# Transposed input, an early first product and adding DMAs in a seven-product projection on Trainium2

## The chip, the cores and the metric

The kernel runs on one core of a Trainium2 chip. The metric is the device time of one execution in microseconds. The core has TensorE (PE, matrix products into PSUM, with the weight load PEld as a row of its own), VectorE (DVE), ScalarE (ACT), GpSimd (POOL) and SyncE (SP). PE adds in eight PSUM banks of 128 x 512 floats. SP, ACT and POOL also issue DMAs; each of these queues is worked off in order, and all transfers run on the same 16 DMA engines.

## The reference

A decoder trunk of two layers over 512 tokens of width 2048, all in float32. Layer 0 is gated linear attention (GLA) with four heads, layer 1 latent attention (MLA) with 16 heads. Each layer is

```python
h = rms_norm(x, g_pre)
y = mixer(h, ...)                # one wide projection of h, attention, gate, w_out
x = x + rms_norm(y, g_post)
```

The change lies mostly in the first projection of layer 0:

```python
proj = h @ w_in                                   # 512 x 2048 times 2048 x 6160
q, k, v, gate, gk_low = jnp.split(proj, ...)      # 1024, 1024, 2048, 2048, 16 columns
gk = gk_low @ w_gk2 + b_gk
log_a = log_sigmoid(gk) / 16                      # the decays, summed up within chunks
```

Scores are made of q and k weighted by the exponents of the summed decays; the scores times v are normed per head, multiplied by silu(gate), and go through `w_out`.

## The kernel before

Every float32 product is made of three in the faster format fp32r: a number is split into a high part (rounded on ACT) and a low part (the rest, on DVE), and `mm3` (lines 128 to 132) adds high x high, low x high and high x low into one bank.

The wide projection is cut into six blocks m of 1024 columns, two halves n1 and n2 of 512 each: (q, k) of heads 0 and 1, (v, gate) of heads 0 and 1, then the same for heads 2 and 3. Each block is one 2 x 2 block product with seven multiplications instead of eight. The two halves on the side of x are the token halves and, within each pair kp of 128-row pieces of the 2048, the even and the odd piece; on the side of the weights they are the even and odd piece and n1 and n2. The seven products need sums of pieces on both sides. The left sums live in `act_hi` and `act_lo`, in four slots for each pair; the right sums are made anew while the weights stream in.

The slots hold only four of the seven left operands. So there are two stages:

1. `first_four` (line 253): for all six blocks, four products with eight banks, 8 pairs kp of 24 matmuls. SP loads two pieces left (n1) and two right (n2), 512 KB each, three buffers of either; DVE makes three sums, ACT and DVE split four pieces. The results are combined and written to the DRAM tensor `stage` through POOL.
2. `left_rest` (line 374) makes the other left operands from `ht`, the transposed normed input in SBUF.
3. `last_three` (line 286): for each block three products with six banks, 18 matmuls a pair; one reload of `stage` (`done`, 1.5 MB, POOL); the result goes to `evac`. q and k are transposed and multiplied by the decay factors (`qk_evac`, line 579), then `scores` (616), `values` (657) follow for each head. The decays are made by `gk_spread` (510) and `decays` (538) when stage 2 begins and again after the second head.

Before all that, `start` (line 320) loads the rows of x, norms them (ACT squares, DVE scales), transposes them on PE (line 353), copies them to `ht`, splits them, and makes the left sums. `constants` (390) and `gk_low` (498: 32 float32 matmuls of the gate's low rank) follow, then the first block. Results of the heads go through DRAM (`yd`) and are transposed by `gla_rows` (674). `out_proj` (689) makes the output projection in column blocks of 512, the last 512 as two blocks of 256, the second with its weights kept in SBUF; `mla` does the same with the first latent projection (lines 779 to 783: two halves of 256 columns).

The order on each engine comes from a planner: the program is traced, and a scheduler puts each engine's instructions and DMA queue in order by a simulated timeline before it is built (`tc` with `schedule_with_timeline_sim=True`, line 1056). On the chip each queue keeps that order and waits by semaphores. SBUF is handed out by pools that open on the left or on the right side and lie behind one another; a tile that takes over the place of an earlier pool's tile waits until that tile is no longer read.

Of the kernel before, what the change touches and what calls it, by code (L numbers as in the profile page):

```python
# [14 lines left out]
F32 = DT.float32  # L15
# [8 lines left out]
P = 128  # L24
# [21 lines left out]
NMAC = 6  # L46
GQ0, GK0, GV0, GG0, GL0 = 0, 1024, 2048, 4096, 6144
# [3 lines left out]
R_BGK, R_GON, R_GQA, R_GKV, R_PRE = 0, 8, 12, 16, 20  # L51
NROWS = 36
# [23 lines left out]
class Trunk:  # L76
# [121 lines left out]
    def build(self):  # L198
        tc, a = self.tc, self.a
        from contextlib import ExitStack  # L200
        with ExitStack() as ctx:
# [18 lines left out]
            self.gla_rows()  # L220
# [18 lines left out]
    def raw_pair(self, w, c0, kp, rows=2, name="raw"):  # L239

        t = self.wp.tile([P, rows, 512], F32, tag=f"{name}{rows}", name=name, bufs=3)
        src = w[(2 * kp + 2 - rows) * P:(2 * kp + 2) * P, c0:c0 + 512]
        self.nc.sync.dma_start(t, src.rearrange("(k p) n -> p k n", p=P))
        return t

    def prods(self, ps, kp, slots, hi, lo, ws):
        for q, (slot, wi) in enumerate(zip(slots, ws)):
            for r in range(2):
                self.mm3(ps[2 * q + r], self.act_slot(self.act_hi, kp, slot, r),
                         self.act_slot(self.act_lo, kp, slot, r), hi[:, wi, :], lo[:, wi, :],  # L250
                         kp == 0, kp == KT // 2 - 1)

    def first_four(self, w, m, n1, n2):


        nc, v = self.nc, self.nc.vector
        ps = [self.ps.tile([P, 512], F32, tag="a", name=f"pa{q}", bufs=8) for q in range(8)]
        for kp in range(KT // 2):
            r1 = self.raw_pair(w, n1, kp, name="left")
            r2 = self.raw_pair(w, n2, kp, name="right")  # L260
            t = self.wp.tile([P, 3, 512], F32, tag="sums", name="sums", bufs=2)
            v.tensor_tensor(t[:, 0, :], r1[:, 0, :], r2[:, 0, :], ALU.add)
            v.tensor_tensor(t[:, 1, :], t[:, 0, :], r2[:, 1, :], ALU.add)
            v.tensor_tensor(t[:, 2, :], t[:, 1, :], r1[:, 1, :], ALU.add)
            hi = self.wp.tile([P, 4, 512], FR, tag="w_hi", name="w_hi", bufs=2)
            lo = self.wp.tile([P, 4, 512], FR, tag="w_lo", name="w_lo", bufs=2)
            nc.scalar.copy(hi[:, 0, :], r1[:, 0, :])
            v.tensor_tensor(lo[:, 0, :], r1[:, 0, :], hi[:, 0, :].bitcast(F32), ALU.subtract)
            nc.scalar.copy(hi[:, 1:4, :], t)  # L269
            v.tensor_tensor(lo[:, 1:4, :], t, hi[:, 1:4, :].bitcast(F32), ALU.subtract)  # L270
            self.prods(ps, kp, (0, 2, 1, 3), hi, lo, (0, 2, 1, 3))
        for r in range(2):
            p1 = self.stg([P, 512], "p1")
            nc.scalar.copy(p1, ps[r])  # L274
            nc.gpsimd.dma_start(self.stage[m, :, 0, r, :], p1)
            u = self.stg([P, 512], "u2")
            v.tensor_tensor(u, p1, ps[2 + r], ALU.subtract)
            for i, p in ((1, ps[4 + r]), (2, ps[6 + r])):
                t = self.stg([P, 512], "vw")
                v.tensor_tensor(t, u, p, ALU.add)  # L280
                nc.gpsimd.dma_start(self.stage[m, :, i, r, :], t)

# [3 lines left out]
    def last_three(self, w, m, n1, n2, evac):  # L286


        nc, v = self.nc, self.nc.vector
        ps = [self.ps.tile([P, 512], F32, tag="b", name=f"pb{q}", bufs=6) for q in range(6)]  # L290
        done = self.sp.tile([P, 3, 2, 512], F32, tag="done", name="done", bufs=1)
        nc.gpsimd.dma_start(done, self.stage[m])
        for kp in range(KT // 2):
            r1 = self.raw_pair(w, n1, kp, 1, name="left")
            r2 = self.raw_pair(w, n2, kp, name="right")
            t = self.wp.tile([P, 512], F32, tag="sum", name="sum", bufs=2)
            v.tensor_tensor(t, r2[:, 0, :], r2[:, 1, :], ALU.add)
            hi = self.wp.tile([P, 3, 512], FR, tag="w_hi", name="w_hi", bufs=2)
            lo = self.wp.tile([P, 3, 512], FR, tag="w_lo", name="w_lo", bufs=2)
            for i, x in enumerate((r1[:, 0, :], r2[:, 1, :], t)):  # L300
                nc.scalar.copy(hi[:, i, :], x)
                v.tensor_tensor(lo[:, i, :], x, hi[:, i, :].bitcast(F32), ALU.subtract)  # L302
            self.prods(ps, kp, (2, 0, 1), hi, lo, (0, 1, 2))
        for r in range(2):
            p2, q3, p7 = ps[r], ps[2 + r], ps[4 + r]
            c = [self.stg([P, 512], f"c{i}") for i in range(4)]
            v.tensor_tensor(c[0], p2, done[:, 0, r, :], ALU.add)
            evac(r, 0, c[0])
            v.tensor_tensor(c[1], q3, done[:, 1, r, :], ALU.subtract)
            evac(r, 1, c[1])  # L310
            v.tensor_tensor(c[2], p7, done[:, 2, r, :], ALU.add)
            evac(2 + r, 0, c[2])
            v.scalar_tensor_tensor(c[3], p7, -1.0, done[:, 1, r, :], ALU.mult, ALU.subtract)
            evac(2 + r, 1, c[3])
# [5 lines left out]
    def start(self):  # L320

        nc, v, a, cp = self.nc, self.nc.vector, self.a, self.cp
        xs = a["x"][0]
        tc = self.tc
        cf = cp.tile([P, P + 1], F32, name="cf")
        self.ident, self.invf = cf[:, 0:P], cf[:, P:P + 1]
        self.eps = cp.tile([P, 1], F32, name="eps")
        nc.vector.memset(self.eps, EPS)
        self.junk = cp.tile([P, 512], BF16, name="junk")
        with tc.tile_pool(name="start", bufs=1, reuse_waits="tile") as xp:  # L330
            xt = []
            for s in range(ST):
                x = xp.tile([P, D], F32, tag="x", name=f"x{s}", bufs=3)
                for g in range(4 if s == 0 else 1):
                    c = slice(g * 512, (g + 1) * 512) if s == 0 else slice(0, D)
                    nc.sync.dma_start(x[:, c], xs[s * P:(s + 1) * P, c])
                if s == 0:
                    nc.scalar.dma_start(cf, a["consts"])
                    gr = xp.tile([P, D], F32, tag="grow", name="grow")
                    nc.scalar.dma_start(gr, a["l0_pre_norm"][None, :].to_broadcast([P, D]))  # L340
                xt.append(x)
            for s in range(ST):
                parts = self.st.tile([P, 4], F32, tag="parts", name="parts", bufs=2)
                for g in range(4):
                    self.sumsq(xt[s][:, g * 512:(g + 1) * 512], parts[:, g:g + 1])
                rstd = self.rstd_of(self.total(parts, "x_ssq"), D, "x_rstd")
                cols = slice(s * P, (s + 1) * P)
                for g in range(4):
                    c = slice(g * 512, (g + 1) * 512)
                    v.scalar_tensor_tensor(xt[s][:, c], xt[s][:, c], rstd, gr[:, c], ALU.mult, ALU.mult)  # L350
                    pt = self.ps.tile([P, 512], F32, tag="a", name="xn_t", bufs=8)
                    for j in range(4):
                        nc.tensor.transpose(pt[:, j * P:(j + 1) * P],
                                            xt[s][:, (4 * g + j) * P:(4 * g + j + 1) * P], self.ident)
                    pv = pt.rearrange("p (k n) -> p k n", n=P)
                    nc.scalar.copy(self.ht[:, 4 * g:4 * g + 4, cols], pv)
                    ks = slice(4 * g + s // 2, 4 * g + 4, 2)
                    self.split_from(pv[:, s // 2::2, :], self.act_hi[:, ks, cols], self.act_lo[:, ks, cols])
            for g in range(4):
                self.left_sums(xp, g)  # L360

    def left_sums(self, pool, g):

        nc, v = self.nc, self.nc.vector
        h = lambda odd, half: self.ht[:, 4 * g + odd:4 * g + 4:2, half * 256:(half + 1) * 256]
        x = pool.tile([P, 2, 2, 256], F32, tag="lsum", name="lsum", bufs=2)
# [5 lines left out]
        v.tensor_tensor(sl(self.act_lo), x, sl(self.act_hi).bitcast(F32), ALU.subtract)  # L372

    def left_rest(self, g):

        nc, v = self.nc, self.nc.vector
        h = lambda odd, half: self.ht[:, 4 * g + odd:4 * g + 4:2, half * 256:(half + 1) * 256]
        x = self.tp.tile([P, 2, 2, 256], F32, tag="lsum", name="lsum", bufs=2)
        v.tensor_tensor(x[:, :, 0, :], h(1, 1), h(0, 1), ALU.subtract)
# [81 lines left out]
    def gla(self):  # L461
# [8 lines left out]
        with pool("ht", **R) as hp:  # L470
# [9 lines left out]
            with pool("lb", **R) as self.tp:  # L480
                for g in range(4):
                    self.left_rest(g)
# [577 lines left out]
```

## Time and profile before

| | |
|---|---|
| median of 3 runs | 1564.92 us (1564.27 to 1565.75) |
| the profiled execution, its span | 1565.73 us, 1564.0 us |
| first product matmul of `first_four` | 72.7 us |
| last product matmul of `first_four` | 337.3 us |
| heads done, transposes of `gla_rows` begin | 656 us |
| granted PE clock, mean | 0.967 |
| DMA | 216.09 MB, mean 138 GB/s |

The page of the profile has busy times by engine, the span in 40 slices, the queues, the chain of work that ended last, and groups of equal instructions. A window row gives, for a stretch of the span, the busy time of each engine with its number of instructions, the granted PE clock, the mean busy share of the DMA engines, and what they moved. Matmuls overlap in the records: one of 512 columns is shown as 0.39 us, though a new one starts every 0.23 us. So the rate is the stretch divided by the number of matmuls. A wait row names who waited for what: total, times, longest. A group's row ends with the idle time ahead of it and what ended it. A DMA row has the median time from issue to landing.

### The profile page before, as it was taken

How to read it: one execution, taken by the hardware profiler on the slowest of the kernel's cores; microseconds unless marked ns; L12 is line 12 of the kernel's file. 1: busy time of each engine (PE TensorE's matmuls, PEld its weight loads, DVE VectorE, ACT ScalarE, POOL GpSimd, SP SyncE). 2: the span in 40 equal slices, each digit the busy share in tenths (PEclk: the TensorE clock that was granted, in tenths of full speed). 3: DMA queues.
4: the chain of work that ended last, by engine and by line, in shares of the span. 5: the costliest groups of instructions: out<-in, count | busy, mean ns of one | idle time of the engine just before them, and what ended most of it. 6: DMA issues, size and time to landing. Idle time of an engine off the chain costs nothing.

```text
span 1564.0 us, 19919 instructions
## 1 busy us (share of the span) xinstructions
PE 1463.3 (94%) x7409; PEld 1234.4 (79%) x7409; DVE 978.1 (63%) x1652; ACT 729.7 (47%) x1391; POOL 68.6 (4%) x130
## 2 busy tenths in 40 slices
PE   2699999978699799699999999999999999999998
PEld 2287887857588678588899988888888889888888
DVE  6488888879888878544347434344367777863324
ACT  6233343335366446534336424444466666753221
POOL 0200000001000000200001100000000000000000
PEclk7799999999899989799999999999999999999999
DMA  7167777745366555744326223333322221235222
GB/s 283 29 181 223 229 226 226 223 166 188 121 199 192 167 168 163 256 132 126 111 88 227 71 81 105 98 95 94 82 72 70 60 60 51 69 124 171 94 95 108
DMA packets 132961, 216.09 MB, mean 138 GB/s; under 512 B 19628, under 2 KB 56720, under 8 KB 130048
## 3 DMA queue, kind: packets, MB, share of 16 engines
q1 hardware_dynamic: 124064, 178.81, 37.4%
q0 software_dynamic: 8512, 34.89, 6.5%
q8 instruction: 58, 0.95, 0.3%
q10 hardware_dynamic: 288, 1.11, 0.2%
q14 instruction: 39, 0.32, 0.1%
HBM read 192.53 MB, written 22.25 MB: 137 GB/s over the span
## 4 chain that ended last, share of the span: by engine, by line
PE 70%; issue 18%; DVE 6%; DMA 3%; ACT 2%; POOL 1%; SPq 0%; DVEq 0%; POOLq 0%; ACTq 0%
PE yo_acc L130 8%; PE yo_acc L132 8%; PE yo_acc L131 8%; PE pb L130 4%; PE pb L131 4%; PE pb L132 3%; PE acc L132 3%; PE acc L131 3%; PE acc L130 3%; PE q_acc L132 1%; PE q_acc L131 1%; PE q_acc L130 1%; PE pt L1012 1%; DMA right<-in_l_gla_w_in_dram 1%; PE cq_acc L131 1%
## 5 line engine op out<-in xcount | busy, mean ns | idle before, releaser
L131 PE MATMUL yo_acc<-w_hi,act_lo 128*128 128x512 f32 (+1 forms) x440 | 154.1, 351 | 0.0
L132 PE MATMUL yo_acc<-w_lo,act_hi 128*128 128x512 f32 (+1 forms) x440 | 153.0, 349 | 0.0
L130 PE MATMUL yo_acc<-w_hi,act_hi 128*128 128x512 f32 (+1 forms) x440 | 152.8, 349 | 0.0
L130 PE MATMUL pa<-w_hi,act_hi 128*128 128x512 f32 x384 | 150.4, 392 | 1.4 <-ACT p L274 1.4
L131 PE MATMUL pa<-w_hi,act_lo 128*128 128x512 f32 x384 | 149.5, 389 | 0.0
L124 DVE SCALAR_TENSOR_TENSOR w_lo<-w_raw,gcol,w_hi 128x512 fp32r<-128x512 f32 (+1 forms) x98 | 64.6, 698 | 106.6 <-ACT w_hi L123 106.5
L130 PE MATMUL pb<-w_hi,act_hi 128*128 128x512 f32 x288 | 116.4, 408 | 12.7 <-ACT act_hi L384 7.6
L132 PE MATMUL pa<-w_lo,act_hi 128*128 128x512 f32 x384 | 118.3, 389 | 0.0
L123 ACT ACTIVATE w_hi<-w_raw,gcol 128x512 fp32r<-128x512 f32 (+1 forms) x98 | 61.5, 676 | 114.0 <-PE acc L132 83.9
L131 PE MATMUL pb<-w_hi,act_lo 128*128 128x512 f32 x288 | 114.0, 397 | 0.0
L132 PE MATMUL pb<-w_lo,act_hi 128*128 128x512 f32 x288 | 101.0, 398 | 0.8 <-DVE w_lo L302 0.8
L130 PE MATMUL acc<-act_hi,w_hi 128*128 128x512 f32 x256 | 99.7, 389 | 0.0
L131 PE MATMUL acc<-act_hi,w_lo 128*128 128x512 f32 x256 | 99.6, 389 | 0.0
L132 PE MATMUL acc<-act_lo,w_hi 128*128 128x512 f32 x256 | 99.1, 389 | 0.0
L270 DVE TENSOR_TENSOR w_lo<-sums,w_hi 128x1536 fp32r<-128x1536 f32 x48 | 84.2, 1754 | 15.1 <-ACT w_hi L269 15.1
L130 PEld LDWEIGHTS yo_acc<-w_hi,act_hi 128*128 128x128 f32 x440 | 83.7, 190 | 10.5 <-ACT act_hi L179 0.2
L131 PEld LDWEIGHTS yo_acc<-w_hi,act_lo 128*128 128x128 f32 x440 | 83.7, 190 | 10.0
L132 PEld LDWEIGHTS yo_acc<-w_lo,act_hi 128*128 128x128 f32 x440 | 83.6, 190 | 10.0
L116 DVE TENSOR_TENSOR w_lo<-w_raw,w_hi 128x1024 fp32r<-128x1024 f32 x32 | 39.2, 1224 | 80.9 <-ACT w_hi L115 80.8
L130 PEld LDWEIGHTS pa<-w_hi,act_hi 128*128 128x128 f32 x384 | 72.0, 188 | 20.5 <-ACT p L274 3.2
L124 DVE SCALAR_TENSOR_TENSOR w_lo<-w_raw,gon,w_hi 128x512 fp32r<-128x512 f32 (+1 forms) x80 | 47.7, 641 | 59.6 <-ACT w_hi L123 59.3
L132 PEld LDWEIGHTS pa<-w_lo,act_hi 128*128 128x128 f32 x384 | 72.1, 188 | 15.0
(331 smaller groups left out, 3636.9 us busy)
## 6 DMA issues: line engine op xcount, KB each, us to landing
right<-in_l_gla_w_in_dram SPq DMA_DIRECT2D x96, 512.0 KB, 4.3
left<-in_l_gla_w_in_dram SPq DMA_DIRECT2D x48, 512.0 KB, 4.7
w_raw<-in_l_mla_w_in_dram SPq DMA_DIRECT2D x47, 512.0 KB, 3.7
w_raw<-in_l_gla_w_out_dram SPq DMA_DIRECT2D x32, 512.0 KB, 4.0
w_raw<-in_l_mla_w_out_dram SPq DMA_DIRECT2D x32, 512.0 KB, 3.6
left<-in_l_gla_w_in_dram SPq DMA_DIRECT2D x48, 256.0 KB, 3.6
done<-stage POOLq DMA_DIRECT2D x6, 1536.0 KB, 7.4
pw_raw<-in_l_mla_w_kvb_dram SPq DMA_DIRECT2D x64, 128.0 KB, 2.6
```

Source lines behind the costliest of these rows:

```text
L116: nc.vector.tensor_tensor(lo, raw, hi.bitcast(F32), ALU.subtract)
L123: nc.scalar.activation(hi[:, kk, :], raw[:, kk, :], AF.Copy, scale=g)
L124: nc.vector.scalar_tensor_tensor(lo[:, kk, :], raw[:, kk, :], g, hi[:, kk, :].bitcast(F32), ALU.mult, ALU.subtract)
L130: t.matmul(out, lh, rh, start=start, stop=False)
L131: t.matmul(out, ll, rh, start=False, stop=False)
L132: t.matmul(out, lh, rl, start=False, stop=stop)
L270: v.tensor_tensor(lo[:, 1:4, :], t, hi[:, 1:4, :].bitcast(F32), ALU.subtract)
L1012: te.transpose(pt[:, o:o + P], probs[i][:, j * P:(j + 1) * P], self.ident)
```

## The change

1. **Input.** The program gets x transposed (`xt`) and all gains as columns, laid out ahead of the launch. `start` loads `xt` by 128-row pieces, even ones first, and multiplies by the gain. The row norm isn't applied to x any more; its factors (`rcol`) are made by `x_norm` after block 0 and are multiplied in where q, k, v and the gate leave the projection, and into the low-rank gate.
2. **Early product.** The first of the seven products (even pieces, first token half, n1) is formed for blocks 0, 1 and 2 by `first_one`, as pieces of `xt` and weights come in, ahead of the left sums. For these blocks `first_four` makes three products, and four for the others.
3. **Adding DMAs.** One sum of weight pieces in either stage is made by a DMA from POOL that adds a 256 KB piece from DRAM onto the loaded one in SBUF.
4. **Order.** `gk_low`, `gk_spread` and the first `decays` come after block 1; the sums for the second stage are made in place in `ht` after block 3 (`left_swap`), so `left_rest` only splits. Both heads' scores follow q and k at once. `stage` is reloaded in pieces of 256 KB. The transposes of the heads move into the second stage (`y_rows`), the last head's straight from SBUF. `ht` moves to the left side of SBUF.
5. **Widths.** The last 512 columns of `out_proj` and the first latent projection are one block of 512 columns, halved along the 2048 instead.

The core of the diff:

```diff
+    def first_one(self, w, n1, rows=None):
+        ps = [self.bank("a", f"p1_{r}") for r in range(2)]
+        wr = w[:, n1:n1 + 512].rearrange("(k p) n -> p k n", p=P)
+        for g in range(4):
+            t = self.wp.tile([P, 2, 512], F32, tag="left", name="left", bufs=3)
...
+            wt = self.split_w(t)
+            for i in range(2):
+                self.prod(ps, 2 * g + i, 0, wt, i)
+        return ps
+    def first_four(self, w, m, n1, n2, p1=None):
+        have = p1 is not None
+        ps1 = None if have else [self.bank("t", f"p1_{r}") for r in range(2)]
+        ps = [self.bank("a", f"pa{q}") for q in range(6)]
+        for kp in range(KT // 2):
+            left = self.raw_pair(w, n1, kp, "left")
+            right = self.raw_pair(w, n2, kp, "right")
+            if DMA_ADD:
+                nc.gpsimd.dma_start(right[:, 0, :], w[2 * kp * P:(2 * kp + 1) * P, n1:n1 + 512], accum_op=ALU.add)
+            else:
+                v.tensor_tensor(right[:, 0, :], left[:, 0, :], right[:, 0, :], ALU.add)
+            v.tensor_tensor(right[:, 1, :], right[:, 0, :], right[:, 1, :], ALU.add)
+            wr = self.split_w(right)
+            v.tensor_tensor(left[:, 1, :], right[:, 1, :], left[:, 1, :], ALU.add)
+            if have:
...
+                nc.scalar.copy(hi[:, 1, :], left[:, 1, :])
+                v.tensor_tensor(lo[:, 1, :], left[:, 1, :], hi[:, 1, :].bitcast(F32), ALU.subtract)
+                wl = hi, lo
+            else:
+                wl = self.split_w(left)
+                self.prod(ps1, kp, 0, wl, 0)
+            self.prod(ps[0:2], kp, 2, wr, 1)
+            self.prod(ps[2:4], kp, 1, wr, 0)
+            self.prod(ps[4:6], kp, 3, wl, 1)
     def last_three(self, w, m, n1, n2, evac):
-        nc.gpsimd.dma_start(done, self.stage[m])
         for kp in range(KT // 2):
+            t = self.wp.tile([P, 3, 512], F32, tag="raw", name="raw", bufs=3)
...
+            if self.dma_add:
+                nc.gpsimd.dma_start(t[:, 1, :], w[odd, n2:n2 + 512], accum_op=ALU.add)
+            else:
+                v.tensor_tensor(t[:, 1, :], t[:, 1, :], t[:, 2, :], ALU.add)
+            wt = self.split_w(t)
...
+        def done(i, r):
+            t = self.sp.tile([P, 512], F32, tag="done", name="done", bufs=4)
+            nc.gpsimd.dma_start(t, self.stage[m, :, i, r, :])
+            return t
     def start(self):
+        def even(k):
+            nc.sync.dma_start(self.ht[:, k, :], xt[:, k, :])
+            nc.scalar.activation(self.act_hi[:, k, half], self.ht[:, k, half], AF.Copy, scale=gain(k))
+            v.scalar_tensor_tensor(self.act_lo[:, k, half], self.ht[:, k, half], gain(k),
+                                   self.act_hi[:, k, half].bitcast(F32), ALU.mult, ALU.subtract)
+        p1 = [self.first_one(w, self.order[0][0], even)]
+        for g in range(4):
+            ks = slice(4 * g + 1, 4 * g + 4, 2)
+            nc.sync.dma_start(self.ht[:, ks, :], xt[:, ks, :])
+        for m in (1, 2):
+            p1.append(self.first_one(w, self.order[m][0]))
+            for g in (2 * m - 2, 2 * m - 1):
+                for k in range(4 * g, 4 * g + 4):
+                    nc.scalar.activation(self.ht[:, k, :], self.ht[:, k, :], AF.Copy, scale=gain(k))
+                self.left_sums(g)
+    def x_norm(self):
+        for s in range(ST):
+            for g in range(4):
+                t = self.tmp([P, 512], F32, "x")
+                nc.gpsimd.dma_start(t, self.a["x"][0, s * P:(s + 1) * P, g * 512:(g + 1) * 512])
+                self.sumsq(t, parts[:, s, g:g + 1])
...
     def gla(self):
+            with pool("ht") as hp, pool("wa") as self.wp, pool("psa", space=PS) as self.ps:
+                    early = [self.p1_out(m, ps) for m, ps in enumerate(early)]
                     for m, (n1, n2) in enumerate(order):
+                        self.first_four(w, m, n1, n2, early[m] if m < len(early) else None)
+                        if m == 0:
+                            self.x_norm()
+                            self.constants()
+                        if m == 1:
+                            self.gk_low()
+                            self.gk_spread()
+                            with tc.issue_after(self.ln_exp.ins):
+                                self.decays(0)
+                        if m == 3:
+                            for g in range(4):
+                                self.left_swap(g)
+                    for g in range(4):
+                        self.left_rest(g)
+                for p in range(2):
+                    self.last_three(w, 3 * p, *qk(p), self.qk_evac)
+                    at = [self.scores(h) for h in (2 * p, 2 * p + 1)]
+                    if p == 0:
+                        self.decays(1)
+                    for i, h in enumerate((2 * p, 2 * p + 1)):
+                        self.last_three(w, 3 * p + 1 + i, *vg(h), self.vg_begin(h))
+                        if h == GH - 1:
+                            for e in range(h):
+                                self.y_rows(e)
+                        self.values(h, at[i])
+                self.y_rows(GH - 1)
     def out_proj(self, w, gpost, y_of, then, ahead=None, gain=None):
-        self.block_s(w, 1536, 256, 0, ps, hi, lo, KT, gain=gain, evac=evac(3, 1536, 256, 0))
-        self.block_s(w, 1792, 256, 256, ps, hi, lo, KT, gain=gain, evac=evac(4, 1792, 256, 256), resident=True)
+        self.block_s(w, 1536, 512, 0, ps, hi, lo, KT, gain=gain, ks=(0, KT // 2))
+        self.block_s(w, 1536, 512, 0, ps, hi, lo, KT, gain=gain, evac=evac(3, 1536, 512, 0), resident=True,
+                     ks=(KT // 2, KT))
```

`split_w` copies a tile to `w_hi` on ACT and subtracts for `w_lo` on DVE; `prod` is the six matmuls of one product for one pair; `bank` hands out six banks of tag "a" and two of tag "t".

More of the change, by code (lines that the diff above doesn't have):

```diff
@@ new lines, in split_w, with prod @@
+    def split_w(self, t):
+        nc = self.nc
+        shape = list(t.shape)
+        hi = self.wp.tile(shape, FR, tag="w_hi", name="w_hi", bufs=self.w_bufs)
+        lo = self.wp.tile(shape, FR, tag="w_lo", name="w_lo", bufs=self.w_bufs)
+        nc.scalar.copy(hi, t)
+        nc.vector.tensor_tensor(lo, t, hi.bitcast(F32), ALU.subtract)
+        return hi, lo
+    def prod(self, ps, kp, slot, wt, i):
+        for r in range(2):
+            self.mm3(ps[r], self.act_slot(self.act_hi, kp, slot, r),
+                     self.act_slot(self.act_lo, kp, slot, r), wt[0][:, i, :], wt[1][:, i, :],
+                     kp == 0, kp == KT // 2 - 1)
@@ new lines, in first_four @@
+    def first_four(self, w, m, n1, n2, p1=None):
+        nc, v = self.nc, self.nc.vector
+        have = p1 is not None
[12 more added lines that the diff above has]
+            if have:
+                hi = self.wp.tile([P, 2, 512], FR, tag="w_hi", name="w_hi", bufs=self.w_bufs)
+                lo = self.wp.tile([P, 2, 512], FR, tag="w_lo", name="w_lo", bufs=self.w_bufs)
+                nc.scalar.copy(hi[:, 1, :], left[:, 1, :])
[7 more added lines that the diff above has]
+            self.prod(ps[4:6], kp, 3, wl, 1)
+        if not have:
+            p1 = self.p1_out(m, ps1)
+        u = []
+        for r in range(2):
+            u.append(self.stg([P, 512], "u2"))
+            v.tensor_tensor(u[r], p1[r], ps[r], ALU.subtract)
+        for i in (1, 2):
+            for r in range(2):
+                t = self.stg([P, 512], "vw")
+                v.tensor_tensor(t, u[r], ps[2 * i + r], ALU.add)
+                nc.gpsimd.dma_start(self.stage[m, :, i, r, :], t)
@@ L317, in tmp0 @@
+        d = [done(1, r) for r in range(2)]
+        for r in range(2):
+            t = c()
+            v.tensor_tensor(t, ps[2 + r], d[r], ALU.subtract)
+            evac(r, 1, t)
+        for r in range(2):
+            p7 = ps[4 + r]
+            t = c()
+            v.tensor_tensor(t, p7, done(2, r), ALU.add)
+            evac(2 + r, 0, t)
+            t = c()
+            v.scalar_tensor_tensor(t, p7, -1.0, d[r], ALU.mult, ALU.subtract)
+            evac(2 + r, 1, t)
     def tmp0(self, shape, dtype, name):
@@ L329, in start @@
         self.junk = cp.tile([P, 512], BF16, name="junk")
[L330 to L360, printed above, removed]
@@ L1050 @@
     given.update(_constants())
+    given.update(_laid_out(given))
     arrays, a = {}, {}
```

299 lines of the change are left out of this document (145 added, 154 removed).

## The prediction

> **What bounds the kernel now.** I read the page first, then windows cut at the stages, then PE's waits, then the timeline and the groups where an edit has a price.
>
> ```profile
> span 1564.0 us, 19919 instructions
> PE 1463.3 (94%) x7409; PEld 1234.4 (79%) x7409; DVE 978.1 (63%) x1652; ACT 729.7 (47%) x1391; POOL 68.6 (4%) x130
> ...
> core 0: us, PE busy (x) PEld busy (x) DVE busy (x) ACT busy (x) POOL busy (x), PEclk, DMA share, GB/s
> 0.00:72.70 72.70, 30.55 (x98) 16.39 (x98) 43.52 (x86) 37.07 (x84) 8.33 (x19) 0.74 0.49 168
> 72.70:337.30 264.60, 263.18 (x1153) 214.97 (x1152) 215.62 (x261) 101.04 (x108) 17.77 (x33) 1.00 0.68 207
> 337.30:356.00 18.70, 7.00 (x15) 4.49 (x16) 14.52 (x24) 5.89 (x9) 2.15 (x4) 0.69 0.46 155
> 356.00:632.00 276.00, 250.67 (x1128) 204.14 (x1128) 230.22 (x388) 147.30 (x289) 18.57 (x34) 0.95 0.56 175
> 632.00:658.00 26.00, 13.46 (x36) 9.07 (x34) 16.62 (x29) 16.41 (x40) 5.76 (x11) 0.68 0.62 220
> 658.00:1564.00 906.00, 898.48 (x4984) 785.33 (x4984) 457.61 (x869) 421.95 (x863) 16.03 (x30) 1.00 0.33 102
> 195.00:234.00 39.00, 39.00 (x173) 31.87 (x172) 33.06 (x41) 15.76 (x17) 3.23 (x6) 1.00 0.73 222
> 1519.00:1549.00 30.00, 30.00 (x252) 30.00 (x252) 13.04 (x26) 6.88 (x19) 0.00 (x0) 1.00 0.18 66
> 4.00:24.00 20.00, 5.74 (x26) 5.34 (x27) 9.44 (x18) 13.85 (x41) 0.00 (x0) 0.90 1.02 399
> ```
>
> TensorE (PE) bounds it wherever it is fed. The first four products of all six blocks (72.7 to 337.3) run 1152 matmuls in 264.6 us, 0.2297 us each, at full clock. From 658 on PE is also full. The loose time is in three places: the start (72.7 us), the change of stage at 337, and the second stage to 658. The waits name them.
>
> ```profile
> PE xn_t L353 <- DVE x L350: 27.4, 4, 13.0
> PE qk_t L584 <- DVE eq L588: 23.2, 4, 11.0
> PE pb L130 <- ACT act_hi L384: 7.6, 1, 7.6
> PE y_t L683 <- DMA y<-yd: 4.3, 1, 4.3
> ...
> 337.30:354.70 17.40, 5.74 (x12) 3.43 (x12) 0.00 (x0) 0.70 0.49 167
> 384.00:416.00 32.00, 13.10 (x49) 9.41 (x47) 5.20 (x8) 0.79 0.24 73
> 530.00:560.00 30.00, 13.22 (x53) 9.69 (x52) 4.67 (x7) 0.77 0.29 95
> ```
>
> The last three rows count only the product matmuls (pb). Twelve are worth 2.8 us of the 17.4, so 14.6 us are lost at the change of stage. The other two windows hold 49 and 53, worth 11.3 and 12.2; even with some 4 us of transposes in each, about 17 and 14 us are lost, where the decays are computed between q, k and the scores.
>
> **The change, part by part.** The profiled execution took 1565.7 us, 1.7 over its span and 0.8 over the median of the runs; the sum is made against it.
>
> *Start.* Row norms, transposes of x and their waits leave the path. x^T is 4.2 MB (16 x 128 x 512 x 4 bytes), the weights of one early product 2.1 MB, so 10.5 MB come before block 0's own weights: 26 us at the 399 GB/s of 4 to 24 us. PE needs 3 x 48 x 0.2297 = 33.1 us for the three early products and so hides that.
>
> ```profile
> x<-in_x_dram SPq DMA_DIRECT2D x4, 256.0 KB, 7.6
> L267 ACT CAST w_hi<-left 128x512 fp32r<-128x512 f32 x48 | 29.9, 624 | 103.6 <-PE pa L131 103.6
> L268 DVE TENSOR_TENSOR w_lo<-left,w_hi 128x512 fp32r<-128x512 f32 x48 | 33.1, 689 | 38.8 <-ACT w_hi L267 27.0 <-PE pa L131 8.1 <-PE pa L132 2.5
> L274 ACT COPY p<-pa 128x512 f32<-128x512 f32 x12 | 7.0, 581 | 30.9 <-DMA stage<-p 22.2 <-DVE sums L263 4.4 <-PE pa L132 4.3
> 61.42 11.32 PE L504 MATMUL gkl_acc<-ht,gkl_raw 128*16 128x512 f32 x26
> ```
>
> The first matmul waits 7.6 + 0.6 + 0.7 = 8.9 us; with 33.1 and six copies that free the banks (6 x 0.58 = 3.5), block 0 proper starts at 45.5. The gains and the left sums on ScalarE (ACT) and VectorE (DVE) hide under products one and two. The low-rank gate's 32 matmuls of 0.435 us (13.9) and 2 us for the decays move into the stage; half is charged (8), since they fit into the stalls below. The removed transposes were on no full PE.
>
> *Adding DMAs.* Now every pair of row blocks passes through three buffers: load, adding DMA (a), remaining adds, split, release. DVE's add that goes is worth nothing by itself: DVE is busy 215.6 of 264.6 us and PE is full. The new wait sits on POOL: behind an add wait stage writes, reloads and the x loads; for it wait DVE, ACT and PE. On SP the next left load, and the right one behind it, wait for the release.
>
> ```profile
> right<-in_l_gla_w_in_dram SPq DMA_DIRECT2D x96, 512.0 KB, 4.3
> left<-in_l_gla_w_in_dram SPq DMA_DIRECT2D x48, 512.0 KB, 4.7
> gkl_raw<-in_l_gla_w_in_dram POOLq DMA_DIRECT2D x1, 128.0 KB, 4.1
> DMA to landing us min/median/max: 3.4/8.0/11.0
> L115 ACT CAST w_hi<-w_raw 128x1024 fp32r<-128x1024 f32 x32 | 33.7, 1054 | 80.2 <-PE yo_acc L131 76.2 <-DMA w_raw<-in_l_mla_w_out_dram 3.5 <-PE q_acc L132 0.4
> L116 DVE TENSOR_TENSOR w_lo<-w_raw,w_hi 128x1024 fp32r<-128x1024 f32 x32 | 39.2, 1224 | 80.9 <-ACT w_hi L115 80.8
> L269 ACT CAST w_hi<-sums 128x1536 fp32r<-128x1536 f32 x48 | 71.0, 1479 | 22.8 <-DVE sums L264 22.8
> L270 DVE TENSOR_TENSOR w_lo<-sums,w_hi 128x1536 fp32r<-128x1536 f32 x48 | 84.2, 1754 | 15.1 <-ACT w_hi L269 15.1
> ```
>
> No row shows an adding DMA. The nearest are POOL's loads from DRAM: 4.1 us for 128 KB, and 3.4 (shortest) to 8.0 us (median) for the 256 KB loads of x in the output stage, the fourth row. I take a = 5.0, near the lower ones because the 8.0 holds queueing behind siblings, and above them because an add must also fetch what it adds to; 3.4 and 8.0 stay as bounds. A negative price is excluded: the load must land first.
>
> Blocks 0 to 2: 4.7 + a + 0.69 + 1.05 + 1.22 + 0.69 + 0.62 + 0.69 = 9.66 + a, so 14.7 over three buffers, 4.89 us a pair, against 18 x 0.2297 = 4.13 for PE. Blocks 3 to 5 split one piece more on each engine: 10.6 + a = 15.6, 5.2 against 24 x 0.2297 = 5.51, hidden. The stage then ends at 45.5 + 24 x 4.89 + 24 x 5.51 + 8 = 303.1 instead of 337.3: **-34.2**.
>
> The Trainium skill ("DMA: Bandwidth & Descriptors", Anatomy of one DMA) fits a DMA from GpSimd as 2.0 us plus bytes over 436e3, an estimate of 2.6 us for 256 KB; the trace's POOL loads are longer. By it the sum would be about 1480.
>
> *Second stage.* Its chain is 4.7 + a + 1.48 + 1.75 = 12.9, 4.31 us a pair against 4.13: 48 x 0.18 = 8.6, half covered by scores and values: **+4**. The decays of heads 0 and 1 move into the first stage, those of 2 and 3 beside v and g. Of the 31 us lost in the two windows I take 26 back; what is late next is the evacuation of q and k, now with a ScalarE scaling, for which the next block's products are the cover: **-26** (bounds -20 and -31). At the end of the stage three of four heads are transposed early and the last comes straight from SBUF: the 4.3 us wait and part of the 26 us window with 36 matmuls go, **-10** (-4 to -15). The change of stage stays: ht now lies on the left, where I read the second stage's weight tiles to be placed, so their loads wait until the last split of ht (1.48 + 1.75) is done; then 4.3 + 5 + 1.48 + 1.75, 15.8 us and a cold clock: **+2** (if the places don't collide -11).
>
> *POOL's queue.* 16 x loads through three buffers and 36 single reloads instead of six stand in it with the adds.
>
> ```profile
> L281 POOL DMA_DIRECT2D stage<-vw x24 | 13.0, 540 | 39.2 <-DVE vw L280 39.2
> POOL done L292 <- DVE c L313: 179.1, 5, 41.0
> ```
>
> Issuing is cheap (0.54 us). But a reload waits for a free buffer, up to 41 us in one piece, and an add behind it would wait along: **+8** (0 to +49, below).
>
> *Wider pieces.* 252 matmuls of 256 columns take 30.0 us (0.1190 each), 173 of 512 take 39.0 (0.2254). 1152 of the first become 576 of the second (768 in the two output projections, 384 in the latent q): 576 x (0.2380 - 0.2254) = **-7.3**.
>
> By the Trainium skill ("TensorE: Matmul & The Clock Gate", Back-to-back issue gap) an isolated warm matmul takes N / 2.4 + 2.5 ns, which leaves 2.5 ns a pair, 1.5 us in all. The trace has 12.6, and weight loads busy all 30.0 of 30.0 us say why. By the rule the sum would be 1508.
>
> Sum: -34.2 - 26 - 10 + 2 + 8 + 4 - 7.3 = -63.5, so **1502 us**.
>
> **Rivals.**
>
> *The add is slow, and the three buffers become the bound (slower).* With a = 8: blocks 0 to 2 cost 17.7 / 3 = 5.89 (+24), blocks 3 to 5 6.2 (+17), the second stage 5.31, uncovered since PE's order is fixed ahead (+53), the change of stage +1: +95 in all, 1597 us. It decides from a of about 7.0. For it: the 8.0 median. Against it: DMA share 0.68 in that stage, and the 128 KB at 4.1.
>
> *Blocked queue.* Adds work, but a reload at the head of POOL's queue holds the next block's first add until the old block is evacuated; PE then waits a + 1.48 + 1.75 = 8.2 us in each of six blocks, 49 instead of 8: 1543. For it: the 179.1 us that POOL waited for that release. Against it: the planner orders each queue by a simulated timeline, in which an add that is ready goes first.
>
> *Cheap add.* a = 3.4 and no blocking: 24 x 0.53 = 13, 4 and 8 us less: 1477. For it: the shortest x load.
>
> **How the numbers follow.** The forecast (1485 to 1525) gets 0.52, the cheap add 0.17, the blocked queue 0.15, the slow add 0.13, and 0.03 is left for a cancellation within 0.2% (3 us), about what a measurement of this kernel can tell. Faster are the first three, 0.84. The range from 1475 to 1560 holds them nearly whole and leaves out the slow add and the rest, about 0.2.
>
> **What would show it.** The first product matmul by 10 us and block 0's own by 45; a pair in blocks 0 to 2 near 4.9 us and in 3 to 5 near 5.5; adds landing in 4 to 6 us; the last first-stage matmul near 303; the 11 us waits of qk_t gone; a gap of some 16 us at the change of stage; no 256-column matmuls in the output projections. Adds of 7 us or more, or SP waiting for the adds' tiles while PE idles all through both stages, would make it wrong.

## The result and the profile after

The changed kernel takes 1629.14 us (median of 4 runs, 1622.57 to 1635.33). The kernel before took 1565.34 us (1564.27 to 1566.08) beside it. The ratio is 1.0408 (95% interval 1.0366 to 1.0449): slower, where the forecast was 1502 us and the range ended at 1560. The profiled execution took 1622.6 us.

The page of the changed kernel, with the totals, the two main DMA queues, the engines' shares of the chain of work that ended last, and loads of the two stages with the median time to landing (`raw` is the second stage's tile; a row from POOLq is an adding DMA):

```profile
span 1620.8 us, 18861 instructions
PE 1479.2 (91%) x6776; PEld 1209.1 (75%) x6776; DVE 890.8 (55%) x1402; ACT 727.7 (45%) x1261; POOL 171.3 (11%) x263
...
q1 hardware_dynamic: 122288, 184.06, 36.9%
q0 software_dynamic: 25152, 63.19, 16.8%
...
PE 62%; DMA 20%; DVE 8%; ACT 5%; issue 4%; SPq 0%; POOL 0%; DVEq 0%; POOLq 0%; ACTq 0%
...
left<-in_l_gla_w_in_dram SPq DMA_DIRECT2D x59, 512.0 KB, 5.8
right<-in_l_gla_w_in_dram SPq DMA_DIRECT2D x48, 512.0 KB, 5.3
...
right<-in_l_gla_w_in_dram POOLq DMA_DIRECT2D x48, 256.0 KB, 5.5
...
raw<-in_l_gla_w_in_dram POOLq DMA_DIRECT2D x48, 256.0 KB, 5.7
```

DVE is relieved as meant. The adds (last two rows) land in 5.5 and 5.7 us, but the loads from SP have become slower too: 5.8 and 5.3 us for left and right, where the kernel before had 4.7 and 4.3. DMA holds 20% of the chain.

Windows of the changed kernel, cut at the first and last product matmul of either stage:

```profile
core 0: us, PE busy (x) PEld busy (x) DVE busy (x) ACT busy (x) POOL busy (x), PEclk, DMA share, GB/s
20.00:40.00 20.00, 19.97 (x59) 7.80 (x58) 18.15 (x27) 19.19 (x35) 2.45 (x5) 1.00 0.72 247
68.80:386.50 317.70, 262.52 (x1028) 205.86 (x1027) 198.64 (x265) 112.55 (x124) 60.96 (x86) 0.91 0.80 211
386.50:402.60 16.10, 0.44 (x3) 0.02 (x1) 4.15 (x6) 2.13 (x3) 5.33 (x9) 0.64 0.90 277
402.60:694.30 291.70, 259.39 (x1145) 208.93 (x1146) 178.55 (x220) 136.43 (x200) 65.97 (x94) 0.96 0.84 221
694.30:1620.80 926.50, 906.09 (x4436) 763.41 (x4434) 467.99 (x857) 430.00 (x853) 20.39 (x38) 0.99 0.33 100
```

The first stage, where PE was full before, now has PE idle for 55 us. The DMA share is 0.80 and 0.84 in the two stages, where it was 0.68 and 0.56. The forecast can be cut in the same way: its second stage is 631.1 (before's last matmul there) - 34.2 + 4 - 26 + 2 + 8 = 584.9, less the 318.9 at which it was to begin. The last column is the first experiment, the same kernel with DVE's sums in place of the adding DMAs.

| part, us | forecast | after | without adding DMAs |
|---|---|---|---|
| start, up to block 0 | 45.5 | 68.8 | 69.5 |
| first stage | 257.6 | 317.7 | 263.0 |
| change of stage | 15.8 | 16.1 | 9.1 |
| second stage | 266.0 | 291.7 | 272.4 |
| rest of the span | 915.6 | 926.5 | 924.4 |
| span | 1500.5 | 1620.8 | 1538.4 |

Of the 120 us between forecast and result, 82 go when the adds go. Of the rest, 24 us are in the start.

PE's waits in the changed kernel (total, times, longest):

```profile
PE pb L131 <- ACT w_hi L252: 43.2, 12, 15.7
PE p L133 <- DVE w_lo L253: 19.1, 8, 5.2
PE p L131 <- ACT w_hi L252: 18.0, 3, 11.3
PE pa L133 <- DVE w_lo L253: 14.8, 7, 3.4
PE pa L131 <- ACT w_hi L252: 13.5, 3, 7.9
...
PE qk_t L676 <- DVE eq L680: 1.3, 1, 1.3
```

PE waits for split weights in every product (p, pa, pb). The wait of the transposes for the decays, 23.2 us before, is 1.3: that part of the change worked. What the splits wait for stands in the critical chain between 193 and 223 us (start, length, what):

```profile
193.30 6.29 DMA right<-in_l_gla_w_in_dram
...
200.15 4.81 DMA right<-in_l_gla_w_in_dram
...
208.01 1.15 DVE w_lo L253
209.16 0.02 issue
209.18 6.39 DMA right<-in_l_gla_w_in_dram
...
216.12 5.94 DMA right<-in_l_gla_w_in_dram
...
222.70 1.23 DVE w_lo L253
```

A load of 6.3 us, the add onto it of 4.8, DVE's sums and the split, whose end releases the buffer, and the next load: 15.9 us round, then 14.8. With three buffers that would be 5.3 and 4.9 us a pair; the stage took 317.7 / 48 = 6.6, so the three buffers did not overlap fully all through the stage.

### The profile page after: what moved, and what is told of

It reads as the page before. It is cut to its first block, busy times and chain, and to the rows that moved or that the text cites. A ratio compares the mean times of both kernels' runs of the same rounds, so it can differ in the third digit from the quotient of the medians.

```text
span 1620.8 us, 18861 instructions
## 1 busy us (share of the span) xinstructions
PE 1479.2 (91%) x6776; PEld 1209.1 (75%) x6776; DVE 890.8 (55%) x1402; ACT 727.7 (45%) x1261; POOL 171.3 (11%) x263
## 3 DMA queue, kind: packets, MB, share of 16 engines
q0 software_dynamic: 25152, 63.19, 16.8%
## 4 chain that ended last, share of the span: by engine, by line
PE 62%; DMA 20%; DVE 8%; ACT 5%; issue 4%; SPq 0%; POOL 0%; DVEq 0%; POOLq 0%; ACTq 0%
DMA right<-in_l_gla_w_in_dram 10%; PE yo_acc L131 7%; PE yo_acc L132 7%; PE yo_acc L133 7%; DMA raw<-in_l_gla_w_in_dram 7%; PE acc L133 3%; PE acc L132 3%; PE acc L131 3%; DVE w_lo L253 3%; ACT w_hi L252 2%; PE pb L131 1%; PE pb L133 1%; PE pb L132 1%; DMA left<-in_l_gla_w_in_dram 1%; PE q_acc L132 1%
## 5 line engine op out<-in xcount | busy, mean ns | idle before, releaser
L131 PE MATMUL yo_acc<-w_hi,act_hi 128*128 128x512 f32 x352 | 138.0, 393 | 1.3 <-ACT w_hi L124 1.3
L132 PE MATMUL yo_acc<-w_hi,act_lo 128*128 128x512 f32 x352 | 137.6, 391 | 0.0
L253 DVE TENSOR_TENSOR w_lo<-raw,w_hi 128x1536 fp32r<-128x1536 f32 x48 | 83.7, 1755 | 96.5 <-ACT w_hi L252 96.4
L133 PE MATMUL yo_acc<-w_lo,act_hi 128*128 128x512 f32 x352 | 136.1, 389 | 0.0
L252 ACT CAST w_hi<-raw 128x1536 fp32r<-128x1536 f32 x48 | 70.5, 1476 | 113.0 <-DMA raw<-in_l_gla_w_in_dram 69.7
L125 DVE SCALAR_TENSOR_TENSOR w_lo<-w_raw,gcol,w_hi 128x512 fp32r<-128x512 f32 x89 | 63.3, 747 | 101.9 <-ACT w_hi L124 101.8
L252 ACT CAST w_hi<-right 128x1024 fp32r<-128x1024 f32 x48 | 50.4, 1049 | 142.3 <-DVE right L298 70.2
L133 PE MATMUL pa<-w_lo,act_hi 128*128 128x512 f32 x288 | 100.6, 415 | 14.8 <-DVE w_lo L253 14.8
L124 ACT ACTIVATE w_hi<-w_raw,gcol 128x512 fp32r<-128x512 f32 x89 | 59.7, 716 | 111.4 <-PE acc L133 83.9
L131 PEld LDWEIGHTS pb<-w_hi,act_hi 128*128 128x128 f32 x288 | 56.9, 197 | 63.8 <-ACT w_hi L252 48.3
L125 DVE SCALAR_TENSOR_TENSOR w_lo<-w_raw,gon,w_hi 128x512 fp32r<-128x512 f32 x64 | 45.1, 748 | 85.2 <-ACT w_hi L124 85.2
L298 DVE TENSOR_TENSOR right<-right 128x512 f32<-128x512 f32 x48 | 33.0, 688 | 103.0 <-DMA right<-in_l_gla_w_in_dram 103.0
L117 DVE TENSOR_TENSOR w_lo<-w_raw,w_hi 128x1024 fp32r<-128x1024 f32 x32 | 39.2, 1224 | 82.3 <-ACT w_hi L116 82.2
```

What stands on the lines that cost most here:

```text
L117: nc.vector.tensor_tensor(lo, raw, hi.bitcast(F32), ALU.subtract)
L124: nc.scalar.activation(hi[:, kk, :], raw[:, kk, :], AF.Copy, scale=g)
L125: nc.vector.scalar_tensor_tensor(lo[:, kk, :], raw[:, kk, :], g, hi[:, kk, :].bitcast(F32), ALU.mult, ALU.subtract)
L131: t.matmul(out, lh, rh, start=start, stop=False)
L132: t.matmul(out, ll, rh, start=False, stop=False)
L133: t.matmul(out, lh, rl, start=False, stop=stop)
```

## The experiments

Theory A: the add stands in the tile's way, and three buffers don't cover it. Rival B: not the adds but the new order (early product, row norm, gate) costs the time. Rival C: the adds load the DMA engines and slow every other transfer.

**Without adds, and with adds in one stage.**

```diff
-DMA_ADD = True
+DMA_ADD = False
```

> Both sums of weight pieces are made by DVE again, no adding DMA at all; the rest of the change stays. Theory A (the wait for the add lengthens the way of a tile through its three buffers, and this way sets the pace): a pair in the first stage falls from 6.6 us to 4.8 (blocks 0 to 2) and 5.5 (3 to 5), the stage from 318 to about 250, the second stage from 292 to about 255, so about 1525 us. Theory B (the changed order at the start, with the x loads and the low-rank gate in front, costs the time, and the adds little): not below 1600. Theory C (the adds cost by their traffic on the DMA engines): as A, the two are told apart by the plain loads.

1539.21 us, ratio 0.9824 (0.9807 to 0.9840): 1.8% below the kernel before. B falls, though A's 1525 isn't reached: the stages fall to 263 and 272 us, not to 250 and 255.

```diff
-        self.dma_add = DMA_ADD
+        self.dma_add = False
```

> Adding DMAs in the first stage only, DVE sums in the second. Theory A: the second stage gains its 35 us, about 1594. Theory B: about 1625.

1599.12 us, 1.0203 (1.0183 to 1.0223).

```diff
-            if DMA_ADD:
+            if False:
```

> Adding DMAs in the second stage only, DVE sums in the first. Theory A: the first stage gains its 70 us, about 1559. Theory B: about 1625.

1571.14 us, 1.0035 (1.0023 to 1.0047). So the adds cost 59.9 us in the first stage and 31.9 in the second; 1539.2 + 91.8 = 1631, and both together measured 1629: the costs add up.

**The same way without accumulating.** Plain loads of the same pieces, onto the same places with the same waits (the sums are thus left out).

```diff
-                nc.gpsimd.dma_start(right[:, 0, :], w[...], accum_op=ALU.add)
+                nc.gpsimd.dma_start(right[:, 0, :], w[...])
-                nc.gpsimd.dma_start(t[:, 1, :], w[...], accum_op=ALU.add)
+                nc.gpsimd.dma_start(t[:, 1, :], w[...])
```

> The adding DMAs become plain loads of the same bytes from POOL onto the same place, with the same waits; this leaves out the sums of the weight pieces. Theory A (the way through the buffers, any load there costs it): within 1% of the changed kernel, 1615 to 1640, landing 5 to 5.5 us instead of 5.5. Theory C (what the adding itself costs the DMA engines): clearly faster, about 1560, with landing near 3.5 us.

1581.35 us, 1.0094 (1.0063 to 1.0126): 42 us over the kernel without adds and 48 under the changed one (its five executions spread from 1574 to 1589). Every engine has its instructions and DMAs in the same order here as in the changed kernel, so the 48 us are the price of accumulating. The 42 are those of a transfer in the tile's way, together with whatever a new order is worth: the planner laid out the kernel without adds anew from PE's 109th instruction on, and no run parts the two. By stages, the first takes 263.0 us without adds, 296.2 with plain loads and 317.7 with adds, the second 272.4, 282.3 and 291.7 (the profiled executions with plain loads and with adds are 34 us apart instead of 48). The POOL queue of the three pages (packets, MB, share of 16 engines over the span) and the landing times say what is different; first this kernel, then the one without adds:

```profile
span 1586.9 us, 18861 instructions
...
q0 software_dynamic: 19008, 63.19, 12.2%
...
left<-in_l_gla_w_in_dram SPq DMA_DIRECT2D x59, 512.0 KB, 5.9
right<-in_l_gla_w_in_dram SPq DMA_DIRECT2D x48, 512.0 KB, 5.1
...
right<-in_l_gla_w_in_dram POOLq DMA_DIRECT2D x48, 256.0 KB, 4.9
...
raw<-in_l_gla_w_in_dram POOLq DMA_DIRECT2D x48, 256.0 KB, 4.2
```

```profile
span 1538.4 us, 18609 instructions
...
q0 software_dynamic: 11328, 38.02, 7.1%
...
left<-in_l_gla_w_in_dram SPq DMA_DIRECT2D x59, 512.0 KB, 4.9
right<-in_l_gla_w_in_dram SPq DMA_DIRECT2D x48, 512.0 KB, 4.5
```

SP's loads are as late beside plain loads (5.9 and 5.1 us) as beside adds (5.8 and 5.3): there it is the transfer more that counts. In engine time that is 0.122 x 1586.9 x 16 = 3098 us against 1748, or 14.1 us for each of the 96 loads of 256 KB. The changed kernel has 0.168 x 1620.8 x 16 = 4357, or 27.2 for each add: twice as much at the same 63.19 MB. The Trainium skill ("Collectives: The Full Stack", The bandwidth ceiling: the fold count and why AG ≠ RS ≠ AR) says of the adds made by the DMA engines in a collective that they need two source reads, a descriptor for each, and so get about half the bandwidth of a copy. The rows here, of an add onto SBUF, agree with it: 27.2 / 14.1 = 1.9. The prediction thought of the second fetch when it chose a, the add's own latency, but not as load on the engines.

**Wait or load?** The buffers for these need room, so the split weights have three buffers instead of four (`w_bufs`), and all five leave the second stage to DVE. The base without adds:

> Control: no adding DMAs, three instead of four buffers of split weights in the first stage. If these buffers do not matter, 1539 as with four; if PE lives on them, up to 10 us more.

1556.42 us, 0.9950 (0.9933 to 0.9968); the missing split buffer costs 17 us. With the adds in the first stage:

> Control: adds in the first stage only, three buffers of weight pieces, three of split ones. If the split buffers do not matter, 1599 as with four of them.

1609.97 us, 1.0287 (1.0270 to 1.0305): 53.6 over the base. A fourth buffer for `left` and `right`:

```diff
-        t = self.wp.tile([P, 2, 512], F32, tag=name, name=name, bufs=3)
+        t = self.wp.tile([P, 2, 512], F32, tag=name, name=name, bufs=4)
```

> Adds in the first stage only, with four buffers each for the left and the right weight pieces (and three for split ones). Theory A: the way of a tile, about 19.9 us (3 x 6.6), spreads over four buffers, 5.0 us a pair, so the stage loses some 45 of its 60 us: about 1555. Theory C: no better than with three, 1590 to 1600.

1588.91 us, 1.0148 (1.0128 to 1.0168). It returns 21 of the 53.6 us: 9 in the start, where `first_one` and the left sums use the same buffers, and 13 in the stage. Loads of left now land in 6.7 us instead of 5.8. So more buffers alone don't cover the add: what is in flight then lands later. Now the opposite: DVE makes the sums, and adds of the same size go onto three scratch tiles that nobody reads.

```diff
-                nc.gpsimd.dma_start(right[:, 0, :], w[...], accum_op=ALU.add)
-            else:
-                v.tensor_tensor(right[:, 0, :], left[:, 0, :], right[:, 0, :], ALU.add)
+                nc.gpsimd.dma_start(self.scr[kp % 3], w[...], accum_op=ALU.add)
+            v.tensor_tensor(right[:, 0, :], left[:, 0, :], right[:, 0, :], ALU.add)
```

> First stage only: DVE makes the sums, and the adding DMAs of the same size run beside onto three scratch tiles that no engine reads or waits for; second stage without adds; three instead of four buffers of split weights to make room. Theory A (the wait inside the way through the buffers costs the 60 us of the first stage): near its control, 1539 to 1550. Theory C (the adding loads the DMA engines so that all loads land later): near the kernel with the adds in the first stage, 1585 to 1600.

1588.13 us, 1.0142 (1.0127 to 1.0158): 31.7 us over the base, and no engine waits for them. But nothing holds these adds back either. They are issued from 6.0 to 180.4 us, 17 of the 48 before block 0, where the changed kernel's run from 39.7 to 364.2 with 3 before block 0. Of the 31.7 us, 15 are in the start (block 0 at 82.3 instead of 67.3), 15 in blocks 0 and 1, and next to none behind them, when the adds are over. So the run shows that the load of crowded adds costs time, not how much of the changed kernel's loss is load. And plain loads in the place of these adds:

> As e5 (adds onto scratch tiles that nobody reads, 1588.1, 31.7 us over the same kernel without them), but with plain loads of the same 48 pieces in place of the adds. If the time that the engines spend decides (14.1 against 27.2 engine-us a piece), about half of the 31.7 is left: 1571 to 1575. If it is the extra transfer as such that delays the others, as much as an add: 1583 to 1590. If accumulating alone is what hurts: 1556 to 1562.

1562.77 us, 0.9990 (0.9976 to 1.0005): 6.3 over the base, less than the halved engine time let expect, and all of it in the start (block 0 at 74.1); blocks 0 to 2 take 128.4 us against the base's 129.9. The order on every engine is that of the scratch adds, so the other 25 us are accumulating alone. Why, three windows of the first-stage products (pa) over the same stretch show (PE busy and matmuls, clock, DMA share, GB/s): the scratch adds, the scratch loads, the base.

```profile
67.00:120.00 53.00, 30.95 (x115) 0.90 1.00 276
```

```profile
67.00:120.00 53.00, 40.23 (x164) 1.00 0.95 326
```

```profile
67.00:120.00 53.00, 45.34 (x182) 0.97 0.74 228
```

With free adds the engines are full and move less; the plain loads still fit beside the weights. So in this kernel the engine time of the plain loads was to spare, and that of the crowded adds wasn't. Last, the changed kernel itself with less to move: in blocks 0 to 2 the even left piece, which the add fetches again, is not loaded.

```diff
+            if have:
+                left = self.wp.tile([P, 2, 512], F32, tag="left", name="left", bufs=3)
+                nc.sync.dma_start(left[:, 1, :], w[(2 * kp + 1) * P:(2 * kp + 2) * P, n1:n1 + 512])
+            else:
+                left = self.raw_pair(w, n1, kp, "left")
```

> After with its adding DMAs, but in blocks 0 to 2 the even left piece is no longer loaded (256 KB for each of 24 pairs, which nobody reads there once the add brings its own copy): 6.3 MB less. Theory C (load on the DMA engines decides half of the loss): 24 x 14.1 engine-us are 21 us of all 16 engines; where the engines are 90% busy some 10 to 20 us come back, 1609 to 1619. Theory A alone (the tile's way through three buffers): the add waits for right, not for left, nothing shortens, 1625 to 1632.

1631.66 us, 1.0427 (1.0407 to 1.0447): nothing came back. Over the same stretch the changed kernel and this one show:

```profile
68.80:220.00 151.20, 120.24 (x468) 92.94 (x466) 102.49 (x154) 56.79 (x69) 33.34 (x48) 0.91 0.88 238
```

```profile
68.80:220.00 151.20, 120.59 (x470) 92.32 (x469) 103.29 (x158) 58.14 (x72) 33.24 (x47) 0.90 0.79 197
```

The DMA share falls from 0.88 to 0.79, and PE gets the same number of matmuls. So in blocks 0 to 2 of the changed kernel the round through the buffers (A) paces the stage, not the share of the engines (C). But these blocks hold the smaller part of the loss. The first stage in two, blocks 0 to 2 and 3 to 5, of the changed kernel and of the one without adds:

```profile
68.80:214.60 145.80, 117.90 (x459) 91.33 (x457) 100.14 (x151) 56.43 (x68) 31.91 (x46) 0.91 0.87 235
214.60:386.50 171.90, 144.62 (x570) 114.53 (x570) 98.50 (x115) 56.12 (x56) 29.04 (x40) 0.91 0.74 190
```

```profile
69.50:198.20 128.70, 112.15 (x450) 84.86 (x450) 115.03 (x177) 56.95 (x69) 11.89 (x23) 0.95 0.72 221
198.20:332.50 134.30, 131.56 (x570) 106.20 (x570) 112.01 (x136) 55.66 (x56) 9.68 (x18) 1.00 0.65 197
```

Blocks 0 to 2 lose 17.1 us, blocks 3 to 5 lose 37.6, and there the DMA share is only 0.74. Plain loads in the tile's way take 135.7 and 160.5 us for the two parts: 7 of the 17.1 and 26 of the 37.6. So most of the loss comes with a plain load to wait for already (or with the new order). How much of the rest is later landing and how much load isn't shown, since no run has the changed kernel's adds at their pace without the wait.

**The start.** Without adds it is as late as with them, and PE is busy from 20 to 40 us. What with, the trace says: the planner has put the gate's 32 matmuls, the loads and squares of x, and the sums for the second stage (`left_swap`) ahead of the early products of blocks 1 and 2. First attempt, by the planner's order (and the second kernel likewise for `gk_low`):

```diff
+                            with tc.issue_after(self.mark.ins):
                                 self.x_norm()
```

> All three sums by DVE, as in e1 (1539.2), and the row norm held back: the 16 loads of x (4.2 MB) and their squares are issued only after block 0's results are combined. Theory S1 (the start is bound by transfers, and the loads of x stand ahead of the weights): 4.2 MB at the 300 to 400 GB/s of the first 70 us are 10 to 14 us, so block 0 begins at 55 to 60 instead of 69.5 and the time is 1526 to 1531. Rival S2 (the start is bound by the splitting and by the order of PE's instructions, and x only fills gaps): block 0 begins at 67 to 70, the time stays at 1537 to 1541.

> As e7_hold_x, and the low-rank gate (32 matmuls in float32, 14 us of PE between 17 and 39 us) is held back until block 1's results are combined. If PE had nothing else to do in that time (S1: it waits for weights anyway), the 14 us come back later at full price: block 0 at the place of e7_hold_x or earlier by up to 3 us, and the time 5 to 14 us above e7_hold_x. If they stand in the way of the early products (S2), block 0 begins up to 14 us earlier than in e7_hold_x and the time is equal or a few us below it.

1541.59 us, 0.9848 (0.9830 to 0.9865), and 1540.56 us, 0.9846 (0.9831 to 0.9861). They tell nothing of the theories: x was still loaded from 1.2 us on and the gate still ran from 17 us; the edit held nothing back. Second attempt, by data: the tile that is loaded is first written from a value that an earlier block leaves.

```diff
+            if r == 1 and m < 2:
+                self.mark = self.st.tile([P, 1], F32, tag=f"mark{m}", name=f"mark{m}")
+                v.tensor_copy(self.mark, u[1][:, 0:1])
...
+        v.tensor_copy(raw[:, 0, 0:1], self.mark)
         nc.gpsimd.dma_start(raw, a["l0_gla_w_in"][:, ...])
```

> All three sums by DVE, as in e1 (1539.2). The earlier attempt to hold the low-rank gate back by the planner's order had held nothing: its matmuls still ran from 17 to 36 us and x was still loaded first. Here its weights wait for a value that block 1 leaves, so its 32 matmuls (14 us of PE) and, behind them, the sums for the second stage (12 x 0.69 us of DVE before 42 us) cannot come before that. Theory S2 (they stand ahead of the early products on PE, DVE and ACT): block 0 begins at 54 to 62 instead of 69.5, the 14 us of PE come back later in part, time 1526 to 1538. Rival S1 (the start waits for weights whatever stands there): block 0 stays at 66 to 70 and the 14 us are added in the stage, time 1545 to 1555.

1540.43 us, 0.9839 (0.9824 to 0.9853). Block 0 begins at 60.1 us, as S2 expected, but the time is that of the first experiment, not S2's 1526 to 1538. With x held back in the same way:

> As e10g, and the 16 loads of x (4.2 MB) with their squares wait for a value that block 0 leaves. If the transfers bound the start (S1), block 0 begins 10 us earlier than in e10g; if PE, DVE and ACT do (S2), 0 to 4 us earlier, the 13 us of ACT for the squares being most of it. In either case part comes back when the loads of x then stand beside block 1: time between 12 us less and 4 us more than e10g.

1536.29 us, 0.9817 (0.9802 to 0.9833). Block 0 begins at 51.6 us, 8.5 earlier than in the last run: nearer to S1's 10 than to S2's 0 to 4, though the run doesn't part the loads of x from the 13 us of ACT for their squares. Windows of this kernel, cut 1 us ahead of that:

```profile
0.00:50.50 50.50, 36.86 (x140) 29.30 (x141) 31.56 (x41) 35.47 (x50) 3.63 (x12) 0.97 0.84 286
50.50:331.00 280.50, 258.10 (x1058) 196.98 (x1056) 239.18 (x350) 124.14 (x158) 34.03 (x63) 0.97 0.68 213
```

and of the one without adds:

```profile
69.50:332.50 263.00, 243.71 (x1020) 191.05 (x1020) 227.04 (x312) 112.61 (x124) 21.58 (x41) 0.97 0.68 208
```

By the first matmul of block 0 the start is 18 us shorter and the first stage 16 longer; it ends at 331 instead of 332.5. Of the 16, 9 are the gate: held back alone, it made the stage 272.3 us long (60.1 to 332.4) instead of 263.0, for 13.9 us of matmuls on PE. The planner had filled PE's idle time at the start with work that has to be done anyhow.

**The widths**, as before, without adds: `out_proj` with two blocks of 256 columns, and the latent projection too.

```diff
-        self.block_s(w, 1536, 512, 0, ps, hi, lo, KT, gain=gain, ks=(0, KT // 2))
-        self.block_s(w, 1536, 512, ...)
+        self.block_s(w, 1536, 256, 0, ps, hi, lo, KT, gain=gain, evac=evac(3, 1536, 256, 0))
+        self.block_s(w, 1792, 256, ...)
```

> All three sums by DVE, as in e1 (1539.2), and the last output block and the first latent projection as before (two blocks of 256 columns). The prediction took 7.3 us for the wider pieces: if that is their size, 1546.5 here; if the wider pieces bring little because PE is full in either form, 1539 to 1541.

1543.62 us, 0.9866 (0.9850 to 0.9883). The wider pieces bring 4 us by the medians, 7 by the ratios.

## Why the prediction was wrong

The step that failed is the one on the adding DMAs: "Blocks 0 to 2: 4.7 + a + ... over three buffers, 4.89 us a pair", and "Blocks 3 to 5 ... 5.2 against 24 x 0.2297 = 5.51, hidden". Blocks 0 to 2 took 6.1 us a pair (145.8 / 24). Blocks 3 to 5, where the wait was to cost nothing, took 7.2 (171.9 / 24), and 5.6 without adds: they hold 37.6 of the 54.7 us that the adds cost in this stage. The step failed in three terms, and a itself was the smallest of them.

- **The price of the add.** a = 5.0 was taken and 5.5 measured. The rival of the slow add, 1597 us, "decides from a of about 7.0"; the result was worse than it although a stayed far below (5.7 in the second stage).
- **The old price of everything beside it.** The loads went into the sum with the 4.7 us of before. With 5.8 for left and 5.5 for the add, the rounds are 16.3 and 17.2 us, 5.43 and 5.73 a pair, and the stage 24 x 5.43 + 24 x 5.73 + 8 = 276 instead of 258. (The add waits for right, not left; with right's 5.3 it is 268.) What was missing is that one transfer more makes the others land later, as the plain loads show, and that an add holds the engines for 27.2 engine-us, twice a load. The argument against the slow add, a DMA share of 0.68, overlooked that the adds themselves would raise it, to 0.80.
- **Full overlap.** Dividing the round by three supposes that all three buffers are always on their way. The stage shows 6.6 us a pair, so another 42 us or more aren't in any sum of rounds over three; that these rounds didn't overlap is inferred. That DVE and POOL keep an order laid down ahead, so that one late add holds the splits behind it, fits the trace: DVE's sum behind the add (line 298 of the changed kernel) waited 103.0 us in 29 places for it to land. It was not tested by itself. Nor was the granted clock, 0.91 in this stage against 0.97 without the adds. PE is busy 262.5 us there against 243.7 for as many matmuls, 18.8 of the 54.7 us lost; whether the clock adds to the loss or falls because PE idles stays open.

The other steps:

- **Start and first stage, -34.2.** Block 0 at 45.5 was nearly reached (51.6) only when x and the gate were held back: the sum had the gate in the stage and no loads or squares of x in the start, and the planner put all of these ahead of block 0. "Half is charged (8)" was about right for the gate in the stage, where it cost 9.3 us. PE's 4.13 us a pair wasn't reached in blocks 0 to 2 without adds either: they took 128.7 us, 5.4 a pair, with DVE busy for 115.0. The changes of block were not in the sum at all: in the held-back kernel PE waited 11.9 us for their subtraction (`u`). The early product and the transposed input end the stage at 332.5 without adds, 5 us sooner than before instead of 34.
- **Second stage, +4.** The adds cost 31.9 us here. Worked out as in the prediction, with the 5.7 that the add took to land and 5.4 for the load under it, the round is 14.3 us, 4.78 a pair against 4.13, or 31 us if nothing covers it. So the step took both times too small and counted on cover, though no run shows that there was none.
- **Decays, -26.** The mechanism is right: the wait of 23.2 us is 1.3. But without adds the second stage and its change are 12.3 us shorter than before (332.5 to 614 against 337.3 to 631.1); PE waits 16.2 us there for split weights.
- **Change of stage, +2.** Right: a gap of 16.1 us where 15.8 was worked out, with SP's first load waiting 28.1 us for the last split of `ht`. Without the add in it, 9.1.
- **Blocked POOL queue, +8 or 49.** It didn't happen: POOL waited 28.5 us in seven places for the release of a reload's buffer, the longest 14.2. What POOL waited for most was the loads under its adds, 134.3 us for `raw` and 95.9 for `right`.
- **Tail and widths, -17.3.** The widths were about right (4 to 7 of 7.3). The rest of the span is 8.5 us shorter than before's 932.9 without adds, so some 2 to 4 us are left for the transposes instead of 10.

The kernel without adding DMAs beats both, 1539 against 1565 and 1629; with x and the gate held back it is 1536, not apart from it.

## What to carry to other kernels

A DMA that adds spares an engine a sum and charges the DMA engines twice; where the sum was on an engine that wasn't the limit and the stage streams weights, little is won for something scarce. When a step is put into a buffer's way, price the round with the landing times that the new traffic will cause, and don't divide by the number of buffers unless the trace shows them all in flight. And a start that is shortened is worth only what had no work to fill it.

## What was unexpected of the hardware

- An adding DMA of 256 KB takes 27.2 engine-us against 14.1 for a plain load of the same bytes (23.5 and 11.6 in the scratch kernels), and the queue's MB count it once. It lands in 5.5 us against 4.9 in the first stage and 5.7 against 4.2 in the second, so the latency shows less of the price than the engine time.
- At a DMA share of 1.00, with adds among the loads, 276 GB/s were moved; at 0.95 with plain loads, 326.
- POOL spends 0.86 us on issuing an add and 0.54 on a plain load.
